# A hybrid attention and expert layer on one core: modulation rows in eight places and partly straight to TensorE, two low halves moved from GpSimd to VectorE, a residual load in eight parts

## The chip, the core and the metric

The kernel runs on one core of a Trainium2 chip. The metric is the device time of one execution in microseconds (us). The engines are TensorE (PE; its weight loads are PEld), VectorE (DVE), ScalarE (ACT), GpSimd (POOL) and SyncE (SP, which here only issues DMAs). An engine works through its own instructions in order and waits on semaphores of others.

## What is computed

The reference, cut to the layer's outline (the attention and the short convolution are left out):

```python
mod = (silu(c) @ w_mod + b_mod)                      # 1024 -> 6 x 1024
sh1, sc1, gt1, sh2, sc2, gt2 = split(mod, 6)
h = rmsnorm(x, ln_mix_g) * (1 + sc1) + sh1           # x: 256 tokens x 1024
proj = h @ w_in                                      # 24 column groups go to attention and conv
mixed = concat(rmsnorm(o_attn), rmsnorm(o_conv))
x = x + gt1 * (mixed @ w_out)
h2 = rmsnorm(x, ln_ffn_g) * (1 + sc2) + sh2
q = (h2 @ peer_wq).reshape(256, 8, 2, 64)            # 8 heads
s = einsum('shpd,hpkd->shpk', q, sub_keys)           # two halves of 128 keys each
experts, g = top-16 of the 16 x 16 best sums, softmax
x = x + gt2 * sum_e g_e * gelu(h2 . u_e) * v_e       # 16384 experts
out = rmsnorm(x, ln_final_g)
```

## The kernel before

**Precision.** Every large product is made of three products in a short format: a weight tile `wraw` (128x1024, 512 KB) is split into `whi` (a cast, mostly on ACT, L120) and `wlo` (raw minus hi, L126, on DVE or on POOL in two halves of 512 columns), the activations into `hhi` and `hlo`; PE sums hhi·whi, hlo·whi and hhi·wlo (`prod3`, all through `mm` at L76). All weight tiles come through one list (`put`, L126 to L185 of the code): SP issues the load into a ring of four `wraw` buffers (L94), and a load waits until the buffer's last reader is done. `ahead` keeps up to three tiles split in advance.

**Stages.** Modulation of the first norm (0 to 38 us), projections (to 88), attention and convolution (to 178), the out projection and the second norm (to 198), the queries and top-16 (198 to 228), the u products over all experts (to 630; PE multiplies every expert's row), the gathered v products (630 to 849), the last norm. In the front part a scheduler orders the instructions by estimated times; from the out projection on the order is the program's.

**The front.** The first norm needs two rows of the modulation: scale (j=1) and shift (j=0). For each, eight tiles of `w_mod` (`mod_tile(j, k)`, 128x1024) are multiplied by a column of `cact` (silu(c)) and summed into `macc` on DVE (`gather_mod`, L253 and L255); eight matmuls with one column of ones then sum over the partitions and turn the row into columns (`mod_cols`, L261; an fp32 matmul takes two passes, so a set of eight shows as 16). Tiles k=0 to 7 of j=1 come first, then those of j=0; the last is taken in two pieces (L328). `A1` is the scale (L323, L324), `sh1` the shift (L332). Then ACT writes `hhi` (L336), and the first projection's matmuls (pj<-hhi,whi) start. Beside it PE transposes x (sc<-ident,macc, L297).

**The second norm and the queries.** `modulate2` and `norm_turned` (L760 to L810) add the out projection to x (L764), square it, turn it and write `hhi` and `hlo` (L796). The loads of the eight `wq` tiles (one per head, h=0 to 7) begin before it. For h=0, 1 and 2 the low halves are made by POOL (`low=G`), for the others by DVE. Behind the loads of h=4 and h=5 in SP's order stand the two loads of `pk`, the product keys (L881). PE then makes each head's query (pq<-..., 24 matmuls; the first one's tile is called oT), ACT copies it to `pqs` (L913), and `score` multiplies it by `pk` (pk<-pk,pqs, 8 passes), one head behind. Between `wlo` of h=2 and that copy POOL makes an iota (L884) and a zero tile (L1039) that ACT's queue sends out (L1041).

**The last stage.** POOL issues indirect gathers of 128 rows of v each (L86, DMA_INDIRECT) and gathers of numbers (rows,ixact and rows,ixhalf); ACT and DVE split each tile; PE adds it with `out_tile` (acc<-whi,ah and so on, 128x512). At gather n=60 of this loop SP loads the residual x1 back from DRAM (`x1d`, 128x2048, 1 MB, L1495) and the last norm's gain to all partitions (`row_bias(2, lnf)`, 512 KB); both places are freed by earlier matmuls (the tile `junk`).

Of the kernel before, what the change touches and what calls it, by code (L numbers as in the profile page):

```python
# [58 lines left out]
def layer(nc, tc, d, dbg=None):  # L59
# [23 lines left out]
    lists, room_v = {}, []  # L83
# [4 lines left out]
    def weights(src, n=D):  # L88
        if isinstance(src, int):
            raw = room_v.pop(0)()  # L90
            gather(raw, vrows, lists["v"][:, src:src + 1])
        else:
            raw = wst.tile([128, n], F32, name="wraw", bufs=4)
            Q.dma_start(raw, src)  # L94
        return raw
# [79 lines left out]
    for k in range(1, 4):  # L175
        put(d["w_out"][k])
    for h in range(H):
        put(d["wq"][h], low=G if h < 3 else V)
# [101 lines left out]
    def macc():  # L280
        return f.tile([128, D], F32, name="macc", bufs=4)
# [31 lines left out]
    acc = macc()  # L313
    for k in range(KT_):
        gather_mod(acc, weights(mod_tile(1, k)), k)
    A1 = const.tile([128, KT_], F32, name="A1")
    sh1 = const.tile([128, KT_], F32, name="sh1")
    pA = mod_cols(acc, 0, KT_)
    acc = macc()
    for k in range(KT_ - 1):  # L320
        gather_mod(acc, weights(mod_tile(0, k)), k)
        if k == 4:
            V.tensor_add(A1, pA, vec[:, V_SC1:V_SC1 + KT_])  # L323
            V.scalar_tensor_tensor(A1, A1, 1.0, vec[:, V_G1:V_G1 + 8], op0=OP.add, op1=OP.mult)  # L324
    w = weights(mod_tile(0, KT_ - 1))
    for k0, k1 in ((0, 2), (2, KT_)):
        cs = slice(k0 * 128, k1 * 128)
        V.scalar_tensor_tensor(acc[:, cs], w[:, cs], cact[:, KT_ - 1:KT_], acc[:, cs], op0=OP.mult, op1=OP.add)  # L328
    ahead(1)
    hT = [hp_.tile([128, KT_, T], F32R, name=n) for n in ("hhi", "hlo")]  # L330
    for k0, k1 in ((0, 2), (2, KT_)):
        V.tensor_add(sh1[:, k0:k1], mod_cols(acc, k0, k1), vec[:, V_SH1 + k0:V_SH1 + k1])  # L332
# [526 lines left out]
    run(mod0, mod1)  # L859
    show("x1", xn)  # L860
# [32 lines left out]
    def queries():  # L893
# [11 lines left out]
        for h in range(H):  # L905
            whi, wlo = next_weights()
            p = kps.tile([128, T], F32, name="pq", bufs=2) if h else bank.tile([128, T], F32, name="oT")
            for kk in INTER:
                prod3(p, whi, wlo, kk, kk, kk == 0, kk == KT_ - 1)
            if h:  # L910
                score(q, h - 1)
            q = k.tile([128, T], F32, name="pqs", bufs=2)
            S.copy(q, p)  # L913
            yield
# [572 lines left out]
    for n, q in enumerate(taken):  # L1487
# [6 lines left out]
        if n == 60:  # L1494
            Q.dma_start(x1, x1d)  # L1495
            row_bias(2, lnf)
# [183 lines left out]
```

## Time and profile before

| | |
|---|---|
| median of 3 runs | 873.08 us (870.74 to 875.04) |
| the profiled execution's own time | 869.34 us |
| its span | 867.5 us |
| its mean granted TensorE clock | 0.99 |
| busy: PE, DVE, ACT, POOL | 93%, 74%, 54%, 65% |
| DMA, mean over the span | 230 GB/s |

The profile shows one execution. Durations come from it, and sums are made against its own time; a busy engine is not always the one that sets the end, so the stages are read one by one: which wait ends last there. "Releaser" is the instruction or transfer that the profile names as ending an idle time.

### The profile page before, as it was taken

To read this page: it belongs to the slowest core of one execution; us is meant where nothing else is said; L and a number is where in the kernel's file an instruction comes from. 1 tells how busy PE (TensorE), PEld (TensorE's weight loads), DVE (VectorE), ACT (ScalarE), POOL (GpSimd) and SP (SyncE) were. 2 spreads that over 40 slices of the span, in tenths; PEclk is the share of its full clock that TensorE was granted. 3 is DMA by queue.
4 is the path that set the end of the run, shared out by engine and by line. 5 is a ranking of instruction groups with operands and counts; after the bars stand their busy time and mean duration, and the time that the engine had idled before them with its cause. 6 is when DMAs were issued, how large, how long until landed. Compare 5 with 4: busy or idle time off the path is not lost.

```text
span 867.5 us, 16577 instructions
## 1 busy us (share of the span) xinstructions
PE 809.5 (93%) x5954; PEld 739.4 (85%) x5954; DVE 643.0 (74%) x1555; ACT 470.1 (54%) x911; POOL 565.0 (65%) x504
## 2 busy tenths in 40 slices
PE   3599999989999999999999999999999999899993
PEld 2498888778998989999999999999988887588882
DVE  5746688886998988879979855754456878576676
ACT  4344788555545446555544445544445666466663
POOL 0001485731696966666689887888887777777770
PEclk9999999999999999999999999999999999999997
DMA  8898667425454643466678887889998998887882
GB/s 309 281 235 297 233 220 260 153 90 167 145 177 143 212 151 128 142 179 191 183 210 245 236 264 241 275 272 282 302 321 265 316 342 285 288 296 262 272 252 75
DMA packets 77223, 199.48 MB, mean 230 GB/s; under 512 B 8476, under 2 KB 33021, under 8 KB 76877
## 3 DMA queue, kind: packets, MB, share of 16 engines
q1 hardware_dynamic: 58576, 137.40, 49.8%
q0 software_dynamic: 17456, 59.06, 20.1%
q10 hardware_dynamic: 1100, 1.89, 0.6%
q8 instruction: 49, 0.80, 0.4%
q14 instruction: 42, 0.34, 0.1%
HBM read 179.37 MB, written 18.94 MB: 229 GB/s over the span
## 4 chain that ended last, share of the span: by engine, by line
PE 56%; DMA 17%; POOL 11%; issue 9%; DVE 4%; ACT 3%; SPq 0%; POOLq 0%; ACTq 0%; DVEq 0%
PE ps L76 41%; POOL Bb L86 4%; PE pj L76 4%; DMA wraw<-v,ixv 3%; PE pg L76 3%; POOL wraw L86 3%; DMA mraw<-w_mod 3%; PE pq L76 2%; DMA Ba<-v,ixv 2%; DMA Bb<-rows,ixhalf 2%; DMA Bb<-v,ixv 2%; DMA wraw<-w_mod 1%; DVE macc L255 1%; PE sc L76 1%; DMA wraw<-win 1%
## 5 line engine op out<-in xcount | busy, mean ns | idle before, releaser
L126 POOL TENSOR_TENSOR wlo<-wraw,whi 128x512 fp32r<-128x512 f32 (+1 forms) x242 | 304.4, 1280 | 199.6 <-ACT whi L120 192.9
L76 PE MATMUL ps<-hhi,whi 128*128 128x256 f32 x1024 | 293.1, 286 | 1.0 <-DVE whi L118 1.0
L76 PE MATMUL ps<-hhi,wlo 128*128 128x256 f32 x1024 | 288.6, 282 | 0.8 <-POOL wlo L126 0.8
L76 PE MATMUL ps<-hlo,whi 128*128 128x256 f32 x1024 | 288.6, 282 | 0.0
L120 ACT CAST whi<-wraw 128x1024 fp32r<-128x1024 f32 (+1 forms) x218 | 226.1, 1038 | 84.5 <-PE acc L76 35.5
L126 DVE TENSOR_TENSOR wlo<-wraw,whi 128x1024 fp32r<-128x1024 f32 (+2 forms) x114 | 130.4, 1145 | 87.5 <-ACT whi L120 86.6
L76 PEld LDWEIGHTS ps<-hhi,whi 128*128 128x128 f32 x1024 | 193.1, 189 | 1.6 <-ACT cid L997 1.2
L76 PEld LDWEIGHTS ps<-hhi,wlo 128*128 128x128 f32 x1024 | 193.0, 188 | 1.0 <-POOL wlo L126 1.0
L76 PEld LDWEIGHTS ps<-hlo,whi 128*128 128x128 f32 x1024 | 193.2, 189 | 0.0
L76 PE MATMUL acc<-whi,ah 128*128 128x512 f32 x294 | 94.4, 401 | 3.5 <-ACT whi L120 2.5
L76 PE MATMUL acc<-wlo,ah 128*128 128x512 f32 x294 | 93.6, 398 | 2.1 <-DVE wlo L126 2.0
L76 PE MATMUL acc<-whi,al 128*128 128x512 f32 x294 | 93.3, 397 | 0.0
L1150 ACT ACTIVATE ps<-ps 128x256 f32<-128x256 f32 (+16 forms) x99 | 33.0, 334 | 105.8 <-PE ps L76 103.2
L76 PEld LDWEIGHTS acc<-whi,ah 128*128 128x128 f32 x294 | 55.7, 190 | 18.5 <-ACT whi L120 3.7
L86 POOL DMA_INDIRECT wraw<-v,ixv x53 | 59.5, 1122 | 16.1 <-issue 12.5
L76 PEld LDWEIGHTS acc<-wlo,ah 128*128 128x128 f32 x294 | 55.4, 189 | 16.9 <-DVE wlo L126 4.2
L76 PEld LDWEIGHTS acc<-whi,al 128*128 128x128 f32 x294 | 55.7, 189 | 12.9
L377 POOL TENSOR_TENSOR macc<-macc,mraw 128x256 f32<-128x256 f32 x56 | 47.1, 874 | 26.4 <-ACT mraw L374 26.4
L86 POOL DMA_INDIRECT Bb<-rows,ixhalf x40 | 46.6, 1166 | 11.5 <-issue 10.2
L1089 DVE TENSOR_TENSOR o<-io,keyT 128x1024 f16<-128x1024 f16 x64 | 41.1, 683 | 16.0 <-PE pg L76 13.3
L76 PE MATMUL pj<-hhi,whi 128*128 128x256 f32 x160 | 48.5, 304 | 1.2 <-ACT Y L413 0.5
L76 PE MATMUL pj<-hhi,wlo 128*128 128x256 f32 x160 | 47.1, 295 | 0.0
(364 smaller groups left out, 1453.9 us busy)
## 6 DMA issues: line engine op xcount, KB each, us to landing
wraw<-ut SPq DMA_DIRECT2D x128, 512.0 KB, 4.0
mraw<-w_mod SPq DMA_DIRECT2D x24, 512.0 KB, 4.3
wraw<-win SPq DMA_DIRECT2D x20, 512.0 KB, 4.9
wraw<-w_mod SPq DMA_DIRECT2D x16, 512.0 KB, 5.2
rows<-Bb SPq DMA_DIRECT2D x11, 384.0 KB, 6.1
wraw<-w_out SPq DMA_DIRECT2D x8, 512.0 KB, 4.6
wraw<-wq SPq DMA_DIRECT2D x8, 512.0 KB, 5.1
Bb<-w_mod SPq DMA_DIRECT2D x8, 512.0 KB, 7.1
```

Of the source, the lines that this page charges most:

```text
L76: E.matmul(out, lhsT, rhs, start=start, stop=stop)
L86: G.indirect_dma_start(out=out, out_offset=None, in_=rows, in_offset=bass.IndirectOffsetOnAxis(ap=ix, axis=0))
L120: in_order(S.copy(hi, raw))
L126: ins = eng.tensor_sub(lo[:, cs], raw[:, cs], hi[:, cs].bitcast(F32))
L255: return V.scalar_tensor_tensor(acc, w, cact[:, k:k + 1], acc, op0=OP.mult, op1=OP.add)
L377: G.tensor_add(accs[j][:, cs], accs[j][:, cs], w[:, cs])
L1089: V.tensor_tensor(out.rearrange("p n (m b) -> p n m b", b=2), a, doubled(b).unsqueeze(2).to_broadcast(sh), op=op)
L1150: S.activation(p[:, :n], p[:, :n], AF.Gelu_apprx_tanh)
```

## The change

**Front.** The 16 tiles of `w_mod` get eight places instead of four: four `wraw`, two `mraw` and two halves of `Wb`, used twice. Tiles k=3 and k=7 of each row no longer go through DVE: PE multiplies them itself, eight one-column matmuls (two passes each) with the column of `cact`, into the same PSUM columns as the ones-matmuls. The shift's PSUM columns stand in two tiles, `pj` (2) and `pt` (6).

**Second norm.** The low halves of `wq` h=0 and h=1 are made by DVE, after both halves of the second norm (`split_late`); h=2 stays with POOL. The queries of heads 0 and 1 first take their hi products (16 each), then their lo products (8 each).

**Last stage.** The residual is loaded in eight parts of 128x256 (rows of 1 KB), one at every third gather from n=60 on; the gain follows at n=84.

```diff
+            raw = places.pop(0)() if places else wst.tile([128, n], F32, name="wraw", bufs=4)
...
+    late = []
+    def split_late(raw):
+        hi, lo = (wst.tile([128, D], dt, name=n, bufs=3) for n, dt in (("whi", F32R), ("wlo", F32R)))
+        S.copy(hi, raw)
+        late.append(lambda: V.tensor_sub(lo, raw, hi.bitcast(F32)))
+        ready.append((hi, lo))
     for h in range(H):
-        put(d["wq"][h], low=G if h < 3 else V)
+        put(d["wq"][h], low=G if h < 3 else V, use=split_late if h < 2 else None)
...
+    Wraw = Wb.rearrange("p h t -> p (h t)").rearrange("p (a n) -> p a n", n=D)
+    ring = [lambda: wst.tile([128, D], F32, name="wraw", bufs=4)] * 4 + \
+        [lambda: f.tile([128, D], F32, name="mraw", bufs=2)] * 2 + [lambda: Wraw[:, 0], lambda: Wraw[:, 1]]
+    places += ring * 2
+    direct = (3, 7)
+    def norm_mod(j, cols, acc):
+        out = [ps.tile([128, k1 - k0], F32, name=tag, bufs=2) for (k0, k1), tag in cols]
+        for k in range(KT_):
+            w = weights(mod_tile(j, k))
+            if k not in direct:
+                in_order(gather_mod(acc, w, k))
+            if k in direct:
+                if k == KT_ - 1:
+                    yield out
+                for p, ((k0, k1), _) in zip(out, cols):
+                    if k == KT_ - 1:
+                        for c in range(k0, k1):
+                            E.matmul(p[:, c - k0:c - k0 + 1], acc[:, c * 128:(c + 1) * 128], ones[:, 0:1], start=False,
+                                     stop=False, skip_group_check=True)
+                    for c in range(k0, k1):
+                        E.matmul(p[:, c - k0:c - k0 + 1], w[:, c * 128:(c + 1) * 128], cact[:, k:k + 1],
+                                 start=k == direct[0] and c == k0, stop=k == KT_ - 1 and c == k1 - 1,
+                                 skip_group_check=True)
+            yield out
...
-    pA = mod_cols(acc, 0, KT_)
+    for pA, in norm_mod(1, (((0, KT_), "pj"),), macc()):
+        pass
+    for k, pS in enumerate(norm_mod(0, (((0, 2), "pj"), ((2, KT_), "pt")), macc())):
...
     run(mod0, mod1)
+    for low in late:
+        low()
...
-        for h in range(H):
-            whi, wlo = next_weights()
+        first = []
+        for h in range(2):
+            whi, wlo = ready.pop(0)
             p = kps.tile([128, T], F32, name="pq", bufs=2) if h else bank.tile([128, T], F32, name="oT")
             for kk in INTER:
-                prod3(p, whi, wlo, kk, kk, kk == 0, kk == KT_ - 1)
+                for n in range(2):
+                    mm(p, whi[:, kk * 128:(kk + 1) * 128], hT[n][:, kk], kk == 0 and n == 0, False)
+            first.append((p, wlo))
+        for h in range(H):
+            if h < 2:
+                p, wlo = first[h]
+                for kk in range(KT_):
+                    mm(p, wlo[:, kk * 128:(kk + 1) * 128], hT[0][:, kk], False, kk == KT_ - 1)
+            else:
...
-        if n == 60:
-            Q.dma_start(x1, x1d)
+        if 60 <= n < 84 and n % 3 == 0:
+            i = (n - 60) // 3
+            cs = slice(i % 4 * 256, i % 4 * 256 + 256)
+            Q.dma_start(x1[:, i // 4, cs], x1d[:, i // 4, cs])
+        if n == 84:
             row_bias(2, lnf)
```

TensorE at the start of the program, before (x is in `macc` for the transposes):

```order
L297 MATMUL sc<-ident,macc 128x128 x16
L76 MATMUL sc<-oneh,rels 128x384
L261 MATMUL pj<-ones,macc 128x1 x16
L76 MATMUL pj<-hhi,whi 128x256 x2
L76 MATMUL pj<-hlo,whi 128x256
```

and now:

```order
L306 MATMUL sc<-ident,macc 128x128 x8
L345 MATMUL pj<-cact,wraw 128x1
L306 MATMUL sc<-ident,macc 128x128 x8
L345 MATMUL pj<-cact,wraw 128x1 x7
L76 MATMUL sc<-oneh,rels 128x384
L342 MATMUL pj<-ones,macc 128x1 x8
L345 MATMUL pj<-cact,Wb 128x1 x8
L345 MATMUL pj<-cact,wraw 128x1 x2
L345 MATMUL pt<-cact,wraw 128x1 x6
L342 MATMUL pj<-ones,macc 128x1 x2
L342 MATMUL pt<-ones,macc 128x1 x6
L345 MATMUL pj<-cact,Wb 128x1 x2
```

Four sets of eight one-column matmuls (two passes each) have come in, one of them among the transposes, the last (six more columns into pt follow) behind the last ones-matmuls and right ahead of the first projection.

SyncE around the loads of the product keys, before, with the semaphores that each waits on (the two wq rows at the top are the loads of h=4 and h=5, the last is h=6's):

```order
L94 DMA wraw_2010<-wq 128x1024 [waits DMAHW0_49,Activation_49,Pool_49]
L94 DMA wraw_2017<-wq 128x1024 [waits DMAHW2_49,Activation_49,Pool_49]
L881 DMA pk_2150<-pk 128x256 [waits DMAHW5_49,DMAHW3_49,DMAHW6_49,DMAHW1_49,DMAHW7_49,DVE_49,PE_49]
L881 DMA pk_2150<-pk 128x768 [waits DMAHW4_49]
L94 DMA wraw_2158<-wq 128x1024 [waits Activation_49,Pool_49]
```

and now:

```order
L94 DMA wraw_2031<-wq 128x1024 [waits DMAHW2_49,DVE_49,Activation_49]
L94 DMA wraw_2036<-wq 128x1024 [waits DMAHW4_49,Activation_49,Pool_49]
L912 DMA pk_2171<-pk 128x256 [waits DMAHW5_49,DMAHW3_49,DMAHW6_49,DMAHW1_49,DMAHW7_49,DMAHW0_49,PE_49]
L912 DMA pk_2171<-pk 128x768
L94 DMA wraw_2179<-wq 128x1024 [waits DVE_49]
```

The order is the same; the waits have moved. The load of h=4 now waits for DVE's first late low half, that of h=5 for the POOL half of h=2 (before: the POOL halves of h=0 and h=1), and h=6 for DVE's second.

GpSimd at the same place, before (the first three rows are h=0, 1 and 2, the last two the first u tiles):

```order
L126 TENSOR_TENSOR wlo_2006<-wraw_1524,whi_2005 128x512 x2
L126 TENSOR_TENSOR wlo_2013<-wraw_1530,whi_2012 128x512 x2
L126 TENSOR_TENSOR wlo_2154<-wraw_1618,whi_2153 128x512 x2
L884 IOTA iof_2160 128x128
L1039 MEMSET zero_2169 128x256
```

and now:

```order
L126 TENSOR_TENSOR wlo_2175<-wraw_1641,whi_2174 128x512 x2
L915 IOTA iof_2181 128x128
L1084 MEMSET zero_2190 128x256
L126 TENSOR_TENSOR wlo_2477<-wraw_2266,whi_2476 128x512 x2
L126 TENSOR_TENSOR wlo_2531<-wraw_2321,whi_2530 128x512 x2
```

GpSimd's first instruction here is now h=2's low half.

## Rows read from the trace of the kernel before

**Rows 1.** The page's head: the span.

```profile
span 867.5 us, 16577 instructions
```

**Rows 2.** Busy time of each engine in stretches of the front: the stretch and its length, then the busy us (and instructions) of PE, PEld, DVE, ACT and POOL, the granted clock, the share of the DMA engines' time and the GB/s.

```profile
20.00:25.00 5.00, 3.58 (x16) 3.49 (x16) 1.33 (x5) 0.00 (x0) 0.00 (x0) 1.00 0.80 313
25.00:30.00 5.00, 0.00 (x0) 0.00 (x0) 4.89 (x4) 0.00 (x0) 0.00 (x0) 1.00 0.74 246
30.00:35.00 5.00, 0.81 (x4) 0.81 (x4) 4.08 (x5) 0.00 (x0) 0.00 (x0) 1.00 0.95 338
```

**Rows 3.** The chain of waits that ended last, in the front: start, us, what.

```profile
20.45 3.59 PE pj L261 x16
...
30.20 5.12 DMA wraw<-win
35.34 1.05 ACT whi L120
...
37.75 0.61 ACT hhi L336
...
38.40 8.08 PE pj L76 x42
```

**Rows 4.** The timeline of PE at the start: start, us, line and operation, out<-in, how many; in brackets the idle time before and its releaser.

```profile
15.40 1.65 PE L76 MATMUL sc<-oneh,rels 33*128 33x384 f32 x2
20.45 3.58 PE L261 MATMUL pj<-ones,macc 128*128 128x1 f32 x16 [3.40 <-DVE macc L255]
34.19 3.71 PE L261 MATMUL pj<-ones,macc 128*128 128x1 f32 x16 [10.16 <-DVE macc L328]
```

**Rows 5.** The same timeline later: two pairs of neighbouring projection matmuls, and the ones-matmuls of the second norm.

```profile
43.30 0.41 PE L76 MATMUL pj<-hhi,whi 128*128 128x256 f32 x1
43.51 0.41 PE L76 MATMUL pj<-hlo,whi 128*128 128x256 f32 x1
...
44.06 0.28 PE L76 MATMUL pj<-hlo,whi 128*128 128x256 f32 x1
44.18 0.28 PE L76 MATMUL pj<-hhi,wlo 128*128 128x256 f32 x1
...
185.10 1.84 PE L261 MATMUL scc<-ones,macc 128*128 128x1 f32 x16
```

**Rows 6.** The groups of instructions by line from 0 to 40 us: line, engine, operation, out<-in, count, then busy us and mean ns of one, then idle time before them and its releasers.

```profile
L255 DVE SCALAR_TENSOR_TENSOR macc<-wraw,cact,macc 128x1024 f32<-128x1024 f32 x13 | 16.7, 1284 | 2.7 <-DMA wraw<-w_mod 2.4
```

**Rows 7.** The timeline of DVE in the second norm and behind it.

```profile
183.29 0.69 DVE L764 TENSOR_TENSOR x<-x,cot 128x512 f32<-128x512 f32 x1
...
186.09 2.62 DVE L764 TENSOR_TENSOR x<-x,cot 128x256 f32<-128x256 f32 x2
...
196.89 0.49 DVE L796 TENSOR_TENSOR hlo<-macc,hhi 128x128 fp32r<-128x128 f32 x2 [0.26 <-ACT hhi L807]
...
203.29 1.23 DVE L126 TENSOR_TENSOR wlo<-wraw,whi 128x1024 fp32r<-128x1024 f32 x1 [2.15 <-ACT whi L120]
```

**Rows 8.** The timeline of POOL there.

```profile
185.75 5.31 POOL L126 TENSOR_TENSOR wlo<-wraw,whi 128x512 fp32r<-128x512 f32 x4 [10.47 <-ACT whi L120]
198.09 2.52 POOL L126 TENSOR_TENSOR wlo<-wraw,whi 128x512 fp32r<-128x512 f32 x2 [7.03 <-ACT whi L120]
```

**Rows 9.** The timeline of ACT there.

```profile
196.95 1.07 ACT L120 CAST whi<-wraw 128x1024 fp32r<-128x1024 f32 x1
...
201.95 0.37 ACT L913 COPY pqs<-oT 128x256 f32<-128x256 f32 x1 [3.94 <-POOL zero L1039]
```

**Rows 10.** The timeline of SP's queue there (DMA issues).

```profile
188.46 2.95 SPq L94 DMA_DIRECT2D wraw<-wq  x2
197.45 0.81 SPq L881 DMA_DIRECT2D pk<-pk  x2
```

**Rows 11.** The tile wraw on SP's queue from 180 to 216 us: the time from issue to landing of a 512 KB load.

```profile
DMA to landing us min/median/max: 4.0/4.3/5.2
```

**Rows 12.** The chain of waits from the first score to the end of the u products: start, us, what.

```profile
202.37 0.71 PE pk L76 x8
203.09 3.05 PE pq L76 x24
...
599.96 29.80 PE ps L76 x251
```

**Rows 13.** Stretches of the last stage, columns as in rows 2.

```profile
750.00:755.00 5.00, 2.60 (x10) 1.80 (x10) 0.54 (x2) 0.73 (x1) 3.85 (x4) 1.00 1.00 360
755.00:760.00 5.00, 4.11 (x11) 2.97 (x12) 3.22 (x4) 2.73 (x5) 3.91 (x4) 0.73 1.02 392
...
680.00:700.00 20.00, 20.00 (x87) 16.20 (x86) 16.50 (x22) 12.70 (x19) 15.51 (x15) 1.00 0.94 319
```

**Rows 14.** DMA issues from 740 to 765 us: out<-in, engine, operation, count, KB each, median us from issue to landing.

```profile
Bb<-x1d SPq DMA_DIRECT2D x1, 1024.0 KB, 8.0
```

**Rows 15.** The timeline of POOL in the last stage, around the residual's load and at its end.

```profile
755.07 0.95 POOL L86 DMA_INDIRECT Bb<-rows,ixhalf  x1 [0.30 <-issue]
...
843.78 0.95 POOL L86 DMA_INDIRECT Bb<-rows,ixhalf  x1 [0.30 <-issue]
```

**Rows 16.** The chain of waits at the end of the last stage: start, us, what.

```profile
843.78 5.17 DMA Bb<-rows,ixhalf
849.18 1.05 ACT whi L120
```

More of the change, by code (lines that the diff above doesn't have):

```diff
@@ L82, in layer @@
     vrows = d["v"].rearrange("a p n -> (a p) n")
-    lists, room_v = {}, []
+    lists, room_v, places = {}, [], []
     def gather(out, rows, ix):
@@ L92, in weights @@
         else:
-            raw = wst.tile([128, n], F32, name="wraw", bufs=4)
+            raw = places.pop(0)() if places else wst.tile([128, n], F32, name="wraw", bufs=4)
             Q.dma_start(raw, src)
@@ L310, in layer @@
     Wb = f.tile([128, H, T], F32, name="Wb")
-    acc = macc()
-    for k in range(KT_):
-        gather_mod(acc, weights(mod_tile(1, k)), k)
+    Wraw = Wb.rearrange("p h t -> p (h t)").rearrange("p (a n) -> p a n", n=D)
[22 more added lines that the diff above has]
+            yield out
     A1 = const.tile([128, KT_], F32, name="A1")
     sh1 = const.tile([128, KT_], F32, name="sh1")
-    pA = mod_cols(acc, 0, KT_)
-    acc = macc()
-    for k in range(KT_ - 1):
-        gather_mod(acc, weights(mod_tile(0, k)), k)
+    for pA, in norm_mod(1, (((0, KT_), "pj"),), macc()):
+        pass
+    for k, pS in enumerate(norm_mod(0, (((0, 2), "pj"), ((2, KT_), "pt")), macc())):
         if k == 4:
@@ L324, in layer @@
             V.scalar_tensor_tensor(A1, A1, 1.0, vec[:, V_G1:V_G1 + 8], op0=OP.add, op1=OP.mult)
[L325 to L328, printed above, removed]
     ahead(1)
     hT = [hp_.tile([128, KT_, T], F32R, name=n) for n in ("hhi", "hlo")]
-    for k0, k1 in ((0, 2), (2, KT_)):
-        V.tensor_add(sh1[:, k0:k1], mod_cols(acc, k0, k1), vec[:, V_SH1 + k0:V_SH1 + k1])
+    for p, (k0, k1) in zip(pS, ((0, 2), (2, KT_))):
+        V.tensor_add(sh1[:, k0:k1], p, vec[:, V_SH1 + k0:V_SH1 + k1])
         for k in range(k0, k1, 2):
@@ L904, in queries @@
         q = None
-        for h in range(H):
-            whi, wlo = next_weights()
+        first = []
+        for h in range(2):
+            whi, wlo = ready.pop(0)
             p = kps.tile([128, T], F32, name="pq", bufs=2) if h else bank.tile([128, T], F32, name="oT")
             for kk in INTER:
-                prod3(p, whi, wlo, kk, kk, kk == 0, kk == KT_ - 1)
+                for n in range(2):
[7 more added lines that the diff above has]
+            else:
+                whi, wlo = next_weights()
+                p = kps.tile([128, T], F32, name="pq", bufs=2)
+                for kk in INTER:
+                    prod3(p, whi, wlo, kk, kk, kk == 0, kk == KT_ - 1)
             if h:
```

## The prediction

> **What bounds the kernel now.** I read the views in this order: the chain of waits for the stages that the change touches, then the stretches and timelines around each step of it, then the groups for durations.
>
> In the front the chain [rows 3] ends in the landing of the first projection's weights: issued at 30.20, landed 5.12 us later, cast by ACT at 35.34, then ACT's `hhi` at 37.75, and TensorE's projection at 38.40. Beside it two sets of ones-matmuls of 3.58 and 3.71 us stand on TensorE, which then stands idle for 10.16 us ahead of the second [rows 4]. The transfers are near their limit but not at it: DMA shares of 0.80, 0.74 and 0.95 from 20 to 35 us leave 1.0 + 1.3 + 0.25 = 2.55 us unused [rows 2].
>
> In the second norm VectorE's add to x costs 0.69 us for 512 columns before GpSimd starts, and 2.62 us for the same columns (two of 256) while GpSimd makes the low halves of heads 0 and 1 from 185.75 to 191.06 [rows 7, 8]. After that the chain is TensorE's: the first score at 202.37, then 3.05 us of queries and a score of 0.65 to 0.71 us per head [rows 12], and at its other end the u products, TensorE without a gap up to 629.75 [rows 12]. So a shift of the first score is a shift of the end.
>
> In the last stage GpSimd issues a gather, idles 0.30 us in "issue", issues the next, and waits for nothing else, also while the residual is loaded [rows 15]. The end hangs on its last gather: issued at 843.78, landed 5.17 us later, split from 849.18 on [rows 16].
>
> **Front.** Off VectorE come four tiles of 1.28 us each [rows 6], and the loads get eight places. By transfers alone the first weights could land 2.55 us earlier, at 32.8. But TensorE gains four sets of eight one-column matmuls. A set like it took 3.58 us at this time of the program [rows 4]. Count TensorE's queue: the transposes end at 15.40 [rows 4]; the direct set of the first k=3 tile adds 3.58 (one pair among the transposes, seven behind them): 18.98; the small product of 1.65 us [rows 4]: 20.63; then, in the order shown above, ones, k=7, k=3, ones and k=7, five sets of 3.58 us: 38.53. The projection started at 38.40 [rows 3]. TensorE, idle before, is now the last to arrive, and what the loads and VectorE win waits for it. Gain: none, 0.1 late by the count. What speaks for a little gain: inputs that stood ready earlier take out small waits behind 38.40; against: the new order holds half the transposes behind the landing of a tile. I take **0**, from +0.4 to -0.6.
>
> **Second norm.** Without GpSimd beside it the add should fall from 2.62 to 0.69 us, so everything up to the last `hlo` (196.89 + 0.49 = 197.38 [rows 7]) comes 1.93 us earlier: 195.45. The cast of head 2 on ACT [rows 9] moves from 196.95 to 195.02 and ends at 196.1. GpSimd's two halves for head 2 (2.52 us [rows 8]) run from 196.2 to 198.7. The catch is SyncE's queue. Before, the keys were issued at 197.45 [rows 10], and with half of 0.81 us for the second issue and 4.3 us to land [rows 11] they arrive at 202.2, just before the score at 202.37: they were all but last already. Now the load of head 5 waits for GpSimd's half of head 2, and the keys stand behind it in the same queue. Head 5's load goes out at 198.8, the keys at 199.2 and 199.6, and they land 4.0 to 4.3 us later [rows 11], at 203.6 to 203.9. The 1.93 us won are not only spent, the first score is 1.2 to 1.5 us late. The query copy that released the score before [rows 9] would be ready 1.9 us earlier and no longer counts. TensorE's own work for heads 0 and 1, 48 matmuls at 0.12 us [rows 5] or 5.8 us from the first `hhi` on, is hidden by that wait.
>
> Bounds: if the keys do not arrive last after all, the full 1.9 us is won. If GpSimd is held up by VectorE's two late low halves (1.23 us each [rows 7], starting at 195.45, so until 197.9), its 2.52 us end at 200.4 and the score is 3.2 late. While both worked, four of GpSimd's halves took 5.31 us, 1.33 each, against 1.26 alone [rows 8]: it was VectorE that was held up. I take **+1.5**, from -1.9 to +3.2.
>
> The Trainium skill (GPSIMD Engine Reference, Key points) says that GpSimd shares its SBUF interfaces with VectorE and contends with VectorE instructions that have two SBUF inputs. The add agrees with it [rows 7, 8], and by that rule the contention does not vanish: each late low half has two SBUF inputs and runs beside head 2's halves.
>
> **Last stage.** While 1.5 MB come in, TensorE does 10 and 11 matmuls in two stretches of 5 us where it did 87 in 20 [rows 13]: 43.5 - 21 = 22.5 matmuls of 0.23 us, 5.2 us lost, partly at a lower granted clock (0.73). The DMA engines are full then (1.00 and 1.02), and the residual takes 8.0 us to land [rows 14]. The parts will not be spread as the loop's numbers suggest: parts 2 to 7 wait for the very matmuls (tile `junk`) that free the place for the single load, and SyncE, which has nothing else to do here, sends them out together. The same bytes press on the same gathers, in rows of 1 KB. And if the loss went, it would not show: GpSimd kept its pace through it [rows 15], and the end waits for the last gather [rows 16]. What could be won is only what TensorE still has to do when that tile is split. I take **-0.2**, from -0.8 to +0.3.
>
> **Sum.** 0 + 1.5 - 0.2 = +1.3 on the profiled execution's 869.34 (its span is 867.5 [rows 1]): 870.6. That execution lies 3.74 us below the median of 873.08, so the forecast on the medians is **874.4**. A measurement of this kernel can tell about 0.5% (4.4 us) from no change; this is within it.
>
> **Rivals.**
>
> *TensorE's clock rises during the one-column matmuls* (faster). In the front its passes run at the lower of its two levels (1.2 GHz): projection matmuls start 0.21 us apart up to 43.51, and 0.12 apart at 44.06 (2.4 GHz) [rows 5]; a ones-set takes 3.58 us there and 1.84 at the higher level [rows 4, 5]; the granted clock stands at 1.00 all the while [rows 2]. The changed program keeps TensorE busy from the transposes to 38 us without a break. If that lifts it to the higher level, its queue no longer ends last and the weights do: landed at 32.8, cast and subtracted (1.05 and 1.23 us) by 35.1, 3.3 us ahead; and the matmuls that ran slowly from 38.40 to 43.6 would save up to half of 5.2. That is -3.3 to -5.9, middle -4.6: 869.34 - 4.6 + 1.5 - 0.2, on the medians 869.8. Against: the transposes and the small product, which end at 17.05, did not lift it (the set at 20.45 was slow), nor did 3.7 us of one-column matmuls at 34.19 [rows 4].
>
> The Trainium skill (TensorE: Matmul & The Clock Gate, What's actually happening) says that the lower clock is the default and that activity releases it, by how busy TensorE has been; by that rule 20 us of back-to-back passes lead to this rival's 869.8 rather than to 874.4. The trace agrees for the projection at 43.6, and not for the transposes.
>
> *The keys are in time*: then the second norm's 1.9 us are won: 869.34 - 1.9 - 0.2, on the medians 871.0.
>
> *TensorE's loss at 750 us does set the end* and the parts remove it: 5.2 us, 869.34 + 1.5 - 5.2, on the medians 869.4. For it: TensorE shows no idle time before and after that stall. Against: GpSimd's pace and the last gather [rows 15, 16].
>
> *Head 2's halves wait for the late low halves* (slower): GpSimd ends at 200.4, the keys land at 205.6, 3.2 us late, and the front's queue on TensorE adds its 0.4: 869.34 + 3.2 + 0.4, on the medians 876.7. It decides from the moment the keys' second issue falls later than 198.1 (202.37 - 4.3): from there each us of lateness is a us of the whole.
>
> **How the numbers follow.** Forecast 0.45, clock 0.2, keys in time 0.15, loss at 750 us 0.07, late halves 0.13. The range leaves out half of the two fast cases and a part of the slowest: 868.0 to 877.0. More than 0.5% faster (below 868.7) is about half of the clock's and of the 750 us case, and what the spread of runs (870.74 to 875.04 before) carries over: 0.2. More than 0.5% slower (above 877.4) is the upper part of the last case: 0.1. Within 0.5%: 0.7.
>
> **What would show it.** Front: TensorE's direct sets at 3.6 us each and the projection at 38 to 39 us would bear out the count; sets of 1.9 us and a projection at 34 to 36 the clock. Second norm: the adds at 0.7 us, the last `hlo` at 195.5, and the first score released by the keys' DMA at 203.6 to 203.9; if ACT's copy releases it at 200.5 the step is wrong. Last stage: the parts issued within a few us of one another near 746, the same dip to some 21 matmuls in 10 us, and the last gather 1.3 us later than before with 5.2 us to land. The prediction fails if TensorE runs at the higher level early, if the keys' loads pass ahead of head 5's, or if GpSimd's gathers change their pace.

## The result and the profile after

The changed kernel is slower: median 882.4 us (876.88 to 885.56, 4 runs) against 872.75 us (870.74 to 875.04, 4 runs), ratio 1.0104 with a 95% interval of 1.0059 to 1.0149. The forecast was 874.4, range 868.0 to 877.0, so the time lies outside the range, 8 us beyond the forecast. The profiled execution took 876.88 us with a span of 874.9, 7.4 us longer than before [rows 1].

The difference can be walked along six points that stand in both traces. The ones-matmuls of the second norm start at 185.10 before and 185.52 after (+0.4); the first score at 202.37 and 205.34 (+3.0); the second score at 206.07 and 211.47 (+5.4); the first gathered product at 639.29 and 646.11 (+6.8); the last gather is issued at 843.78 and 851.25 (+7.5); the end comes at 867.5 and 874.9 (+7.4). So 5 of the 7.4 us arise between the ones-matmuls and the second score, some 20 us of the program. Another 1.4 us arise in the u products, the rest is small.

The timeline of TensorE in the front, after (against [rows 4]):

```profile
19.42 3.57 PE L342 MATMUL pj<-ones,macc 128*128 128x1 f32 x16
22.86 3.55 PE L345 MATMUL pj<-cact,Wb 128*128 128x1 f32 x16
...
30.39 1.01 PE L342 MATMUL pj<-ones,macc 128*128 128x1 f32 x4 [0.57 <-DVE macc L264]
...
34.68 2.70 PE L345 MATMUL pt<-cact,Wb 128*128 128x1 f32 x12
37.24 0.77 PE L76 MATMUL pj<-hhi,whi 128*128 128x256 f32 x2
38.62 0.58 PE L76 MATMUL pj<-hlo,whi 128*128 128x256 f32 x1 [0.60 <-DVE hlo L370]
```

The one-column sets stand on TensorE one behind the other at 3.55 us each, with one wait of 0.57 us for VectorE's last sum, and the last direct one right ahead of the projection. The sets end at 37.38 (34.68 + 2.70); the count had put that end at 38.53. VectorE then adds the shift and writes `hlo`, and the projection, whose first two matmuls start at 37.24, runs through from 38.62 on.

The timelines of VectorE, GpSimd and SyncE's queue in the second norm, after (against [rows 7, 8, 10]):

```profile
186.51 0.75 DVE L793 TENSOR_TENSOR x<-x,cot 128x256 f32<-128x256 f32 x2
...
195.19 0.49 DVE L825 TENSOR_TENSOR hlo<-macc,hhi 128x128 fp32r<-128x128 f32 x2 [0.25 <-ACT hhi L836]
195.60 3.44 DVE L183 TENSOR_TENSOR wlo<-wraw,whi 128x1024 fp32r<-128x1024 f32 x2
```

```profile
196.38 3.80 POOL L126 TENSOR_TENSOR wlo<-wraw,whi 128x512 fp32r<-128x512 f32 x2 [20.41 <-ACT whi L120]
```

```profile
196.88 3.66 SPq L94 DMA_DIRECT2D wraw<-wq  x2
200.77 0.80 SPq L912 DMA_DIRECT2D pk<-pk  x2
201.62 0.53 SPq L94 DMA_DIRECT2D wraw<-wq  x1
```

The contention that the change removes is gone: the two adds take 0.75 us where they took 2.62, and the last `hlo` comes 10.16 us after the ones-matmuls started instead of 12.28. But GpSimd's two halves of head 2 and VectorE's two late low halves now run side by side, and both are stretched: 3.80 us for 2.52, 3.44 for twice 1.23. The view of the tile `wlo` from 195.5 to 200.3 us has them one by one (count, then shortest, median and longest in ns, then first and last start):

```profile
L183 DVE TENSOR_TENSOR wlo<-wraw,whi x2: 1217/1763/2309, 195.6 to 196.7; 128x1024 fp32r<-128x1024 f32 x2
L126 POOL TENSOR_TENSOR wlo<-wraw,whi x2: 1577/1922/2267, 196.4 to 197.9; 128x512 fp32r<-128x512 f32 x2
```

With these starts and durations the four end at about 196.8 (VectorE), 198.0 (GpSimd), 199.0 (VectorE) and 200.2 (GpSimd): in turn, some 1.1 us apart, which is close to what one takes alone (1.23 and 1.26). From 195.60 to 200.18 they take 4.58 us, against 4.98 one behind the other. So the two engines hardly work at the same time here.

The load of head 5 waits for GpSimd until 200.2, and the keys go out behind it at 200.77, 3.3 us later than before. The three rows of SyncE above show the queue: two loads, the keys, the next load.

The chain of waits there, after (against [rows 12]):

```profile
197.92 2.27 POOL wlo L126
...
200.77 4.33 DMA pk<-pk
205.10 0.24 issue
205.34 1.23 PE pk L76 x8
206.57 4.98 PE pq L76 x24
211.54 0.65 PE pk L76 x8
212.19 3.05 PE pq L76 x24
```

and the stretches, columns as in [rows 2]:

```profile
200.00:205.00 5.00, 0.31 (x3) 0.11 (x1) 0.30 (x1) 0.37 (x1) 0.64 (x3) 0.91 0.75 214
205.00:210.00 5.00, 4.66 (x24) 4.47 (x25) 1.54 (x2) 2.82 (x5) 0.00 (x0) 0.50 0.38 154
```

The keys' DMA now releases the first score. TensorE stands idle for 5.03 us, and behind that its granted clock is 0.50: the score takes 1.23 us instead of 0.71, head 2's query 4.98 instead of 3.05. From the second score on the rows are those of before, 5.4 us later.

SyncE's queue and the chain's end in the last stage, after (against [rows 14, 16]):

```profile
745.25 10.52 SPq L1542 DMA_DIRECT2D Bb<-x1d  x8
755.82 0.54 SPq L280 DMA_DIRECT2D Bb<-rows  x1
```

```profile
851.25 4.85 DMA Bb<-rows,ixhalf
```

```profile
760.00:765.00 5.00, 3.33 (x12) 2.10 (x12) 2.16 (x3) 1.33 (x3) 3.89 (x4) 1.00 1.02 391
765.00:770.00 5.00, 4.17 (x11) 2.98 (x12) 4.32 (x6) 3.06 (x6) 3.98 (x4) 0.73 0.95 351
```

The parts go out within 10.5 us, the gain behind them, and TensorE dips as before: 12 and 11 matmuls in two stretches of 5 us, the granted clock 0.73 in the second (before: 10 and 11, and 0.73 [rows 13]). The end hangs on the last gather, as before.

### The profile page after: what moved, and what is told of

Same layout as the page of the kernel before. It is cut to its first block, busy times and chain, and to the rows that moved or that the text cites. A ratio compares the mean times of both kernels' runs of the same rounds, so it can differ in the third digit from the quotient of the medians.

```text
span 874.9 us, 16704 instructions
## 1 busy us (share of the span) xinstructions
PE 828.5 (95%) x6018; PEld 757.0 (87%) x6018; DVE 637.1 (73%) x1552; ACT 470.0 (54%) x911; POOL 561.3 (64%) x500
## 4 chain that ended last, share of the span: by engine, by line
PE 63%; DMA 13%; issue 8%; POOL 8%; DVE 3%; ACT 3%; SPq 0%; POOLq 0%; ACTq 0%; DVEq 0%
PE ps L76 41%; PE pj L76 6%; POOL Bb L86 4%; DMA Bb<-v,ixv 4%; PE pg L76 3%; PE acc L76 3%; DMA wraw<-v,ixv 3%; POOL wraw L86 2%; PE pq L76 2%; DMA mraw<-w_mod 2%; PE pt L76 2%; PE sc L76 2%; DMA Bb<-rows,ixhalf 1%; DVE wlo L126 1%; ACT whi L120 1%
## 5 line engine op out<-in xcount | busy, mean ns | idle before, releaser
L126 POOL TENSOR_TENSOR wlo<-wraw,whi 128x512 fp32r<-128x512 f32 (+1 forms) x238 | 300.8, 1283 | 208.2 <-ACT whi L120 201.5
L120 ACT CAST whi<-wraw 128x1024 fp32r<-128x1024 f32 (+1 forms) x216 | 223.8, 1037 | 81.9 <-PE acc L76 38.9
L76 PE MATMUL pj<-hlo,whi 128*128 128x256 f32 x160 | 46.2, 290 | 0.6 <-DVE hlo L370 0.6
```

The costliest lines, as they stand in the source:

```text
L76: E.matmul(out, lhsT, rhs, start=start, stop=stop)
L120: in_order(S.copy(hi, raw))
L126: ins = eng.tensor_sub(lo[:, cs], raw[:, cs], hi[:, cs].bitcast(F32))
```

## Experiments

The runs were made in several sessions, on chips where the kernel before itself took 871 to 884.5 us; each ratio is to runs of the kernel before on the same chip. One theory (*keys*) says that the loss comes from the second norm's part: product keys stuck in SyncE's queue, and the fall of TensorE's clock behind the wait. Its rival (*elsewhere*) says that it comes from the front's one-column matmuls, from the parted residual, or from falls of the clock at other places.

**The changed kernel again** (after_again), no edit. 

> The changed kernel once more, for its time against the kernel before on the same chip and a second profile. If the late product keys (first score at 205.3 us, 3.0 us later than before, then a clock at half for some 6 us) are the main cost, the ratio is 1.008 to 1.013, and the second profile shows the first score again at 205 to 206 us and the second score 5 to 6 us later than before. If what slowed it is the state of the chip or the chance fall of the clock elsewhere (284 to 292 us and 152 to 160 us in the first profile), the ratio goes toward 1.000 to 1.004 and the second profile has its clock dips at other places.

 Ratio 1.0079 (1.0051 to 1.0108): the loss repeats on another chip.

**The second norm's part undone** (b_undone); front and last stage stay changed.

```diff
-        put(d["wq"][h], low=G if h < 3 else V, use=split_late if h < 2 else None)
+        put(d["wq"][h], low=G if h < 3 else V)
...
-    for low in late:
-        low()
```

and the queries in the old order. 

> The changed kernel with the second norm's part undone (low halves of heads 0 and 1 with GpSimd, queries in the old order); the front's and the last stage's parts stay. If the product keys behind the load of head 5 are the cause, the time comes back to within 0.3% of the kernel before (ratio 0.998 to 1.003), with the front 0 to 0.5 us later. If the front's one-column matmuls or the parted residual are, the ratio stays at 1.007 to 1.012.

 Ratio 1.0015 (0.9984 to 1.0046): without this part no loss can be told from none.

**The second norm's part alone** (b_alone): the kernel before with that part of the diff and nothing else. 

> The kernel before with the second norm's part alone. If the keys are the cause, the ratio is 1.006 to 1.011 (5 to 9 us), the first score at 204.5 to 205.5 us and TensorE at half its granted clock for some us behind it. If the other parts are, the ratio is 0.996 to 1.000, since the contention on VectorE (1.9 us) is gone.

 Ratio 1.0053 (1.0025 to 1.0081): this part alone makes a loss, of 4.7 us by the ratio, near the 5 us that the second score shows, and just under the 1.006 to 1.011 that were expected.

**The keys on ACT's queue** (keys_act), in the changed kernel:

```diff
-        Q.dma_start(pk[:, hh], d["pk"][:, hh])
+        S.dma_start(pk[:, hh], d["pk"][:, hh])
```

> The changed kernel with the two loads of the product keys on ACT's queue, ahead of the cast of head 2, so that they no longer stand behind the load of head 5. If the keys are the cause, the first score comes at 202 to 203 us, released by ACT's query copy, the clock does not fall behind it, and 5 to 6 us of the loss are back: ratio 1.001 to 1.005. If the wait for GpSimd's half of head 2 holds the score by another way (the copy stands behind GpSimd's zero tile), the score comes at 203 to 205 us and the ratio is 1.005 to 1.010.

 Ratio 1.0039 (1.0007 to 1.0070). The timeline of TensorE:

```profile
201.85 0.72 PE L76 MATMUL pk<-pk,pqs 64*128 64x128 f32 x8 [2.15 <-ACT pqs L958]
207.05 0.71 PE L76 MATMUL pk<-pk,pqs 64*128 64x128 f32 x8
```

and the stretch there, columns as in [rows 2]:

```profile
200.00:205.00 5.00, 3.15 (x21) 3.03 (x22) 0.81 (x2) 2.78 (x6) 0.52 (x3) 0.78 0.88 329
```

The keys no longer hold the score; the query copy on ACT does, which stands behind GpSimd's zero tile and so behind head 2's halves. The score comes 16.6 us after the ones-matmuls (19.8 in the changed kernel), yet the second follows only 5.20 us later: 2.15 us of idle time, and against the expectation the clock fell all the same (0.78). By the ratio some 3.5 us of the loss are back, but the interval overlaps that of after_again.

**The clock held up through the wait** (keep_warm), in the changed kernel; the added products are not used:

```diff
+                if h == 1:
+                    spare = kps.tile([128, T], F32, name="pq", bufs=2)
+                    for kk in range(40):
+                        mm(spare, wlo[:, kk % 8 * 128:(kk % 8 + 1) * 128], hT[0][:, kk % 8], True, True)
             else:
                 whi, wlo = next_weights()
-                p = kps.tile([128, T], F32, name="pq", bufs=2)
+                p = spare if h == 2 else kps.tile([128, T], F32, name="pq", bufs=2)
```

> The changed kernel with forty more matmuls of 128x256 on TensorE behind the lo products of heads 0 and 1, into the tile that head 2's query overwrites; their product is not used. They fill the wait for the product keys and change nothing else. If the fall of TensorE's clock behind that wait is a cost of its own, the keys land as late as in the changed kernel (first score some 19.8 us after the ones-matmuls of the second norm), but the second score follows 3.7 us behind the first, not 6.0, and 2 to 2.5 us of the whole come back: ratio to the kernel before 1.005 to 1.007. If the clock falls anyway, or falls for another reason than the idle time, the second score stays 6 us behind and the ratio 1.008 to 1.010.

 Ratio 1.0073 (1.0042 to 1.0105). The timeline of TensorE:

```profile
198.80 5.95 PE L76 MATMUL pq<-hhi,wlo 128*128 128x256 f32 x48
205.06 0.72 PE L76 MATMUL pk<-pk,pqs 64*128 64x128 f32 x8 [0.31 <-DMA pk<-pk]
208.75 0.71 PE L76 MATMUL pk<-pk,pqs 64*128 64x128 f32 x8
```

The keys are as late as ever, but the clock stays: 0.72 us for the score, 3.69 to the second. So of the 5.0 us that the second score lost on the ones-matmuls, 2.4 are the clock's and 2.6 the wait's. The whole does not show the 2.4: the interval is 5.5 us wide.

**All waits of the second norm taken out** (late3_keys), in the changed kernel:

```diff
-        put(d["wq"][h], low=G if h < 3 else V, use=split_late if h < 2 else None)
+        put(d["wq"][h], use=split_late if h < 2 else None)
...
-        Q.dma_start(pk[:, hh], d["pk"][:, hh])
+        S.dma_start(pk[:, hh], d["pk"][:, hh])
```

> The changed kernel with the keys on ACT's queue and head 2's low half on VectorE too, right behind the two late ones, so that neither the keys nor GpSimd's half hold the first score. If the two waits are all that is wrong with the second norm's part, the first score comes 15 us after the ones-matmuls of the second norm (17.3 before, 19.8 in the changed kernel), TensorE's idle time ahead of it is under 1 us, the clock does not fall behind it, and the ratio to the kernel before is 0.994 to 0.999. If the clock falls all the same, or VectorE's three subtractions are late, the ratio is 1.000 to 1.004.

 Ratio 1.0022 (0.9993 to 1.0051), the first score 14.37 us after the ones-matmuls, no idle time ahead of it. The timelines of VectorE and TensorE:

```profile
194.27 2.35 DVE L183 TENSOR_TENSOR wlo<-wraw,whi 128x1024 fp32r<-128x1024 f32 x2
196.53 1.22 DVE L126 TENSOR_TENSOR wlo<-wraw,whi 128x1024 fp32r<-128x1024 f32 x1
```

```profile
198.56 0.71 PE L76 MATMUL pk<-pk,pqs 64*128 64x128 f32 x8
202.25 0.72 PE L76 MATMUL pk<-pk,pqs 64*128 64x128 f32 x8
```

VectorE does three low halves one behind the other in about the time (3.57 us) in which it did two beside GpSimd (3.44). Every sign in the second norm came as expected, yet the ratio did not (0.994 to 0.999): against after_again some 5 us are back, what the second norm's part had cost, but the 2.9 us that the first score gains on the kernel before do not show at the end. late3_alone, below, stands 0.83% lower; the front's and the residual's parts alone show 0.1 to 0.4% of that. Where the rest arises was not settled.

**The same mending in the kernel before** (late3_alone), with the front and the residual as before. 

> The kernel before with the second norm's part mended: heads 0 and 1 late on VectorE, head 2 behind them on VectorE, keys on ACT's queue; front and residual as before. If the first score sets the end, it comes some 14.4 us after the ones-matmuls of the second norm (17.3 before), and the ratio is 0.996 to 0.998. If the last stage takes the gain back or the measurement cannot tell it: 0.998 to 1.002.

 Ratio 0.9939 (0.9911 to 0.9968), the first score 14.36 us after the ones-matmuls. The expectation was 0.996 to 0.998; the gain is larger than the 2.9 us that the score shows, and the interval reaches to it.

**The front's part alone** (a_alone and, in another session, a_alone_2). 

> The kernel before with the front's part alone (eight places, tiles k=3 and k=7 straight to TensorE). By the count of the prediction TensorE's queue ends at 38.5 us and nothing is won: ratio 0.998 to 1.003, the projection running without a break from 38 to 40 us on. If the loads that come earlier help the projections behind it, the ones-matmuls of the second norm (185.1 us before) come 1 to 2 us earlier where the clock does not fall on the way: ratio 0.997 to 1.000.

 Ratio 1.0035 (1.0004 to 1.0066). 

> The front's part alone once more, for its time and a second profile. If direct tiles cost by the start of the projection alone (38 to 40 us, as before), the ratio is 0.998 to 1.002 and the first value of 1.0035 was the edge of its interval. If they bring falls of the clock between 70 and 170 us, this profile shows one again and the ratio is 1.002 to 1.006.

 Ratio 1.0003 (0.9967 to 1.0040). The first ratio lies above both ranges of its expectation, the second does not repeat it. The projection runs through from 39.15 us in the first profile and 37.63 in the second. Both have falls of the granted clock between 70 and 170 us (from 75 and 155 us on in the first, from 89 in the second), but so has the kernel before (from 91).

**The eight places, all tiles through VectorE** (a_places), in the kernel before:

```diff
+        for k in range(KT_):
+            in_order(gather_mod(acc, weights(mod_tile(j, k)), k))
+            if k == KT_ - 1:
+                for p, ((k0, k1), _) in zip(out, cols):
+                    for c in range(k0, k1):
+                        E.matmul(p[:, c - k0:c - k0 + 1], acc[:, c * 128:(c + 1) * 128], ones[:, 0:1], start=c == k0,
+                                 stop=c == k1 - 1, skip_group_check=True)
+            yield out
```

> The kernel before with the eight places of the front, but all sixteen tiles through VectorE (no one-column matmuls of weight tiles on TensorE). If TensorE's queue of slow one-column sets is what eats the gain of the earlier loads, the last ones-matmuls now end near 35 us and the projection starts 3 us earlier than before, at 35 to 36 us: ratio 0.995 to 0.999. If the loads or VectorE set that time anyway: the projection at 38 us and 1.000.

 Ratio 0.9925 (0.9899 to 0.9950). The timeline of TensorE:

```profile
30.69 1.01 PE L326 MATMUL pj<-ones,macc 128*128 128x1 f32 x4 [8.62 <-DVE macc L255]
31.56 2.70 PE L326 MATMUL pt<-ones,macc 128*128 128x1 f32 x12
34.12 0.77 PE L76 MATMUL pj<-hhi,whi 128*128 128x256 f32 x2
```

The last sum is ready at 30.69, one set of ones-matmuls follows, and the projection starts at 34.12 and runs through from 35.50 on. The gain, 6.6 us by the ratio, is larger than expected (0.995 to 0.999) and larger than the 3.7 us by which the first product with `hlo` comes earlier (39.15 before, 35.50 here).

**Only tiles k=3 straight to TensorE** (a_direct3): `direct = (3,)`, the sums over k=7 on VectorE. 

> The front's part alone with only tiles k=3 straight to TensorE; tiles k=7 go through VectorE, so that only the ones-matmuls stand behind the last tile. If it is the one-column sets behind the last tile that make the front late, this projection starts at 35 to 36 us, as with the eight places alone, and the ratio is 0.991 to 0.996. If direct tiles cost by something else too (a changed order behind them, falls of the clock between 70 and 170 us), the start is early and the ratio still 0.996 to 1.002.

 Ratio 1.0004 (0.9971 to 1.0037). The projection runs through from 37.64 on, 2.1 us later than with the places alone, though only the ones-matmuls stand behind the last tile here too. The two timelines of VectorE, this kernel's first:

```profile
29.51 1.28 DVE L255 SCALAR_TENSOR_TENSOR macc<-Wb,cact,macc 128x1024 f32<-128x1024 f32 x1 [2.97 <-DMA Wb<-w_mod]
31.48 1.28 DVE L255 SCALAR_TENSOR_TENSOR macc<-Wb,cact,macc 128x1024 f32<-128x1024 f32 x1 [0.69 <-DMA Wb<-w_mod]
```

```profile
27.53 1.28 DVE L255 SCALAR_TENSOR_TENSOR macc<-Wb,cact,macc 128x1024 f32<-128x1024 f32 x1 [1.01 <-DMA Wb<-w_mod]
29.35 1.28 DVE L255 SCALAR_TENSOR_TENSOR macc<-Wb,cact,macc 128x1024 f32<-128x1024 f32 x1 [0.53 <-DMA Wb<-w_mod]
```

Here the last tiles land later. The expectation of 35 to 36 us is wrong, and the traces show the reason. What SyncE waited for from 8 to 32 us (in total, times, longest), in this kernel and with the places alone:

```profile
SPq L94 <- DMA skew<-sk: 6.4, 1, 6.4
```

```profile
SPq L94 <- DMA skew<-sk: 7.2, 1, 7.2
```

and the chain of waits in this kernel:

```profile
15.01 2.78 PE pj L329 x14
17.78 1.59 PE sc L76 x2
...
19.90 5.54 DMA skew<-sk
...
25.93 5.46 DMA Wb<-w_mod
```

In both kernels the loads of the last tiles (into `Wb`) wait for the landing of the table `skew`, a transfer that ACT issues behind the small product (sc<-oneh,rels). On TensorE that product now stands behind the direct set of the first k=3 tile: it starts at 17.71 and not at 15.08. So the table goes out at 19.90 and not at 17.28, the first of the two loads at 25.50 and not at 23.43, and the projection runs through 2.1 us later. The place of the k=3 tile, which TensorE empties, held SyncE's queue for 5.0 us too, but only until 17.81; the wait for the table came after it.

**The parted residual alone** (c_alone). 

> The kernel before with the last stage's part alone (the residual in eight parts). If TensorE's loss beside the load does not set the end, or the parts go out together anyway: ratio 0.997 to 1.003, with the parts issued within a few us and again a dip of TensorE there. If the loss sets the end and the parts remove it: 0.992 to 0.996. If parts of 1 KB rows crowd the gathers more than the single load: 1.003 to 1.006.

 Ratio 1.0008 (0.9979 to 1.0037): no difference. The stretch in which TensorE loses most beside the load:

```profile
765.00:770.00 5.00, 4.07 (x16) 2.68 (x16) 3.24 (x5) 3.85 (x6) 4.08 (x4) 1.00 1.01 377
```

Here the loss is 0.9 us, with 23 matmuls in the stretch before and the one behind, and the clock does not fall. But the dip does not go by the parts: a_alone, on the same chip and with the single load, has 23 and 21 matmuls in the 10 us from 763 on. And the end hangs on something else in c_alone's profile: its chain runs through TensorE's products up to 854.64 and then through a queue that the profile does not name, not through the last gather.

**The eight places and the mended second norm together** (places_late3), residual as before. 

> The kernel before with the eight places alone in the front (all tiles through VectorE) and the second norm's part with its two waits taken out (keys on ACT's queue, head 2's low half on VectorE); the residual as before. If both gains stand beside each other, 5 to 6 us from the front and 1 to 2.5 us from the second norm: ratio 0.990 to 0.993. If VectorE's three subtractions or a fall of the clock eat the second: 0.992 to 0.995. If the last stage's gathers set the end anyway: 0.997 to 1.000.

 Ratio 0.9946 (0.9919 to 0.9974). The first score comes 9.6 us earlier than in the kernel before (192.75 against 202.37), but not all of it arrives at the end: span 863.3 against 867.5 in the two profiled executions. The kernel is faster than the kernel before; that it beats the places alone (0.9925) or the mended norm alone (0.9939) is not shown, and the two gains, 0.75% and 0.61%, do not add: it shows 0.54%.

The points of the walk above for these runs, from their timelines (us; the scores are told from the start of the second norm's ones-matmuls, the end from the first gathered product):

| kernel | ones-matmuls | first score | second score | first gathered product | to the end |
|---|---|---|---|---|---|
| before | 185.10 | +17.27 | +20.97 | 639.29 | +228.2 |
| changed | 185.52 | +19.82 | +25.95 | 646.11 | +228.8 |
| after_again | 182.14 | +19.73 | +25.73 | 643.65 | +247.1 |
| b_alone | 183.62 | +19.66 | +26.18 | 645.23 | +244.2 |
| b_undone | 182.19 | +17.30 | +20.99 | 637.18 | +246.8 |
| keys_act | 185.26 | +16.59 | +21.79 | 642.54 | +240.3 |
| keep_warm | 185.20 | +19.86 | +23.55 | 641.92 | +234.6 |
| late3_keys | 184.19 | +14.37 | +18.06 | 636.40 | +242.7 |
| late3_alone | 185.58 | +14.36 | +18.04 | 636.81 | +234.9 |
| a_alone | 187.74 | +17.29 | +20.97 | 642.73 | +240.9 |
| a_alone_2 | 185.32 | +17.51 | +21.19 | 641.38 | +234.4 |
| a_places | 179.35 | +17.27 | +20.96 | 634.68 | +245.7 |
| a_direct3 | 181.81 | +17.29 | +20.98 | 636.08 | +229.3 |
| c_alone | 183.88 | +17.28 | +20.97 | 638.87 | +243.6 |
| places_late3 | 178.34 | +14.41 | +18.09 | 631.13 | +232.2 |

The two columns of the scores repeat within some tenths of a us wherever the code there is the same: the second norm's part costs 2.4 to 2.6 us at the first score and 4.8 to 5.2 at the second. The column of the ones-matmuls lies between 182.1 and 187.7 for the kernels with four direct sets, and between 183.6 and 185.6 for the old front. Its spread goes with falls of the granted clock on the way (46 to 178 us). The profiles without one read 183.6 and 183.9 with the old front (b_alone, c_alone), 182.1 and 182.2 with four direct sets (after_again, b_undone), 181.8 in a_direct3, 179.4 and 178.3 with the places alone; the changed kernel's 185.52 has a fall from 153 to 161 us in it. So without a fall the front with direct sets is some 1.6 us ahead here, which the times of the whole do not show. The last column is wide, 228 to 235 us in the sessions where the kernel before took 871 to 873 us and 240 to 247 where it took some 884, whichever part is in.

## Why the prediction was wrong, by its steps

**The front's term was right in size, and its count partly by luck.** TensorE's one-column sets did end last, and the two runs of the part alone (1.0035 and 1.0003) lie around no change, the first leaning to a loss. The direct tiles ate what the places won: without them, 0.9925, in the session of the 1.0035. But the sets ended at 37.38, not at the 38.53 of the count; that the projection ran through from 38.62 is VectorE's 1.24 us behind them, which the count left out. And the queue is not the whole mechanism. Between the places alone (35.50) and the part alone (39.15 in that session) lie 3.65 us. The tiles k=3 alone bring 2.14 of them, because their set delays the small product, the table `skew` and the loads that wait for it; that path stands nowhere in the prediction.

**The second norm's term failed**: it was put at +1.5, and the second score shows +5.0 (+5.4 less the 0.4 that the front brought). The mechanism was the one given (head 5's load waits for GpSimd, the keys stand behind it in SyncE's queue, their DMA releases the first score). Two sizes were off. GpSimd's halves were taken at 2.52 us, on the ground that VectorE had been the one held up before; they took 3.80, since VectorE now worked on the same kind of subtraction beside them and the two took turns. That VectorE had been the one held up before fits this: its two adds are short (0.75 us without GpSimd beside them), so GpSimd had little to wait for, and its four halves were long. That is the rival of the late halves: GpSimd ended at 200.2 (the rival said 200.4) and the first score came 2.5 us late on the ones-matmuls (the rival said 3.2). And the wait was priced as a wait alone. That TensorE comes out of it at half its clock, 2.4 us more, as keep_warm separates, stands nowhere in the prediction, though the clock was one of its subjects in the front. The part's own bounds ended at +3.2. The profiled execution, the fastest of the four, took 876.88 where the sum said 870.6; of these 6.2 us, 3.5 are this term's.

The sentence "a shift of the first score is a shift of the end" is not borne out in general. From the second score to the first gathered product 5.4 us became 6.8. In places_late3 8.2 us were won at the first gathered product and 4.2 at the end, and in a_direct3 3.2 us there, with a ratio of 1.0004.

The sentence of the Trainium skill (GPSIMD Engine Reference, Key points) that was weighed there, on VectorE instructions with two SBUF inputs contending with GpSimd, pointed the right way: 3.44 and 3.80 us side by side against 2.46 and 2.52 apart.

**The last stage's term was right in size**: c_alone is 1.0008. In the changed kernel's profile the dip is there and the last gather sets the end, as forecast; in c_alone's neither holds. The parts went out within 10.5 us, not together; it changed nothing.

**The rival on the clock's rise did not come true, though the clock did rise in half of the profiles.** In the changed kernel's profile the sets ran at 3.55 to 3.57 us to the last, and the projection behind them was slow until 43.4, as before. But in four of the eight profiles with four direct sets (keys_act, keep_warm, late3_keys, a_alone_2) TensorE came out of the transposes at the higher level and lost it again within the ones-set, without a break in its work. keep_warm's first direct set, its first ones-set and the next direct set:

```profile
15.00 1.62 PE L345 MATMUL pj<-cact,wraw 128*128 128x1 f32 x14
17.39 2.71 PE L342 MATMUL pj<-ones,macc 128*128 128x1 f32 x16
19.96 3.55 PE L345 MATMUL pj<-cact,Wb 128*128 128x1 f32 x16
```

What the queue won by that, it spent waiting for VectorE's last sum (2.81 us in keep_warm, 0.57 in the changed kernel): the projection ran through from 37.96, only 0.7 us earlier. The rule of the Trainium skill that was named there (TensorE: Matmul & The Clock Gate, What's actually happening), that activity releases the lower clock, is not borne out for these one-column matmuls: they neither raised the clock nor kept it.

**The keys in time** was refuted by the trace: their DMA released the first score. **TensorE's loss at 750 us** would have brought 5.2 us (0.6%); c_alone's interval leaves no room for that, with most of the loss gone from its profile.

What stays open: the second norm's part alone and the front alone add up to 1.006 to 1.009, the whole measured 1.010 and 1.008. In the profiled execution 1.4 us come from a fall of the clock in the u products, which the kernel before did not have there. Behind 1.0 and 0.85 us of idle time that every kernel has at that place (before: at 278.55 and 279.87) the granted clock of the changed kernel went down:

```profile
285.00:290.00 5.00, 4.72 (x27) 4.72 (x28) 4.90 (x6) 0.47 (x3) 5.00 (x5) 0.66 0.37 110
```

The same fall stands in the profiles of after_again, b_alone, keys_act and a_alone_2, and not in those of keep_warm, late3_keys, late3_alone, b_undone, c_alone, a_alone, a_places or a_direct3; places_late3 has one of the same size at 305 us. Why in the one and not in the other was not settled. Nor was what makes the last stage 228 us long in one execution and 235 in another on like chips; it is as large as the effects looked for. The traces show only where the time sits. On like chips it is in GpSimd's own instructions (busy 161.6 us of this stage before, 168.3 in late3_alone). On the chip where the kernel before takes some 884 us GpSimd also waits between gathers, 2.8 to 4.6 us at the longest in each of its eight profiles; elsewhere no such wait is above 0.6 us.

## What to carry to other kernels

When work moves from one engine to another, follow what each queue behind it now waits for: a load that waits for a buffer holds every load behind it in its queue, here the keys, although nothing in the diff touches them. Price a new wait of TensorE with the clock that it leaves behind, not only by its length: 2.6 us of waiting cost 5.0. And an idle engine is not free room if its work is slow there: eight places alone gave 0.75%, and with the direct tiles on TensorE nothing, because the slow sets held up what stands behind them, down to loads on another engine's queue.

## What the hardware showed that was not expected

- TensorE's granted clock stood at 0.50 behind 5.03 us without work (205 to 210 us of the changed kernel), and had fallen behind 2.15 us in keys_act (0.78 in 200 to 205 us). Behind 1.42 us in the kernel before, the queries ran at 3.05 us a head [rows 12]:

```profile
202.37 0.71 PE L76 MATMUL pk<-pk,pqs 64*128 64x128 f32 x8 [1.42 <-ACT pqs L913]
```

With matmuls in the gap (keep_warm) it stayed at 1.00.
- In the front of four profiles the clock fell from the higher level while TensorE worked through one-column matmuls without a break (keep_warm: busy 4.00 of 4.00 us from 16 to 20).
- GpSimd and VectorE, both subtracting with two SBUF inputs, take turns: 1.90 us a half for GpSimd (1.26 alone) and 1.72 a tile for VectorE (1.22 alone), the four ends some 1.1 us apart.
- In the front the granted clock of the records is not to be trusted by itself. In the changed kernel's profile it reads 1.00 from 16 to 36 us, with sets of 3.55 us. In keep_warm's it also reads 1.00 while the transposes still run slowly (six in 1.54 us in both kernels), then falls, and with sets of the same 3.55 us it reads:

```profile
20.00:24.00 4.00, 4.00 (x20) 4.00 (x21) 2.27 (x3) 0.00 (x0) 0.00 (x0) 0.50 1.02 408
```

The duration of a set (3.55 us or 1.84) tells the level in both.
